# A two-layer hybrid decoder trunk on one core: three normalising steps and two preparation steps change their engine or their place

## The chip, the cores and the metric

The kernel runs on one core of a Trainium2 chip. The metric is the device time of one execution in microseconds (us). TensorE (PE) does matrix products, VectorE (DVE), ScalarE (ACT) and GpSimd (POOL) the elementwise work, and SyncE (SP) issues the transfers. Each engine works through its own list of instructions in order; a wait on one instruction holds everything behind it on that engine.

## What is computed

The reference is a stack of two layers on a sequence of 1024 tokens of width 1024. Layer 0 mixes by an SSD recurrence and MLA attention, layer 1 by GLA and NSA attention; each mixer ends in one output projection, and each layer ends in a SwiGLU FFN. Every sub-layer has the same frame:

```python
for layer in range(DEPTH):
    shift_m, scale_m, gate_m, shift_f, scale_f, gate_f = adaln_modulation(c, *ada[layer])
    h = rmsnorm(x, pre_m) * (1.0 + scale_m) + shift_m
    x = x + gate_m * rmsnorm(mixers[layer](h), post_m)
    h = rmsnorm(x, pre_f) * (1.0 + scale_f) + shift_f
    x = x + gate_f * rmsnorm(swiglu(h, *ffns[layer]), post_f)
```

In layer 0 the mixer projects its input to, among others, a query latent `q_a` (384 wide) and a key-value latent `kv_a` (256 wide); `rmsnorm(kv_a)` is multiplied by `w_kv_b` later, in the MLA attention.

## The kernel before

Tokens are cut into eight tiles of 128. All matrix products are made from two-part numbers: an operand is split into `hi` (rounded to the matmul type, on ACT) and `lo` (the rest, mostly on DVE), and `mm3` issues three matmuls for a product (lines 114, 115 and 116 of the file). PSUM banks are handed out from four small rings: `bk`, `cx`, `sm` and `big`. A scheduler of the language places the instructions of each engine; the program gives it the streams, and `merge` and generators that are advanced with `next` set which step is written next to which.

Four places matter here.

**The latent stage of layer 0** (`mixer0_latent`, L940 to L997). `merge` interleaves two streams by weight: `dense()` makes the query latent by long projections, weight 31, and `kv_norm()` normalises the key-value latent, weight 4. For each half of the tokens `row_bcast` multiplies the identity by four columns of `rkv` on DVE (`diag`, L166) and one matmul with ones (L167) spreads them over the partitions into a bank `sm`; POOL adds the two parts of the latent (`kvn`, L990), DVE multiplies (L991), and ACT and POOL split again.

**The mix and the start of the FFN in both layers** (`mix_tiles`, L1195 to L1229, called by `ffn`). Tile by tile PE makes the output projection into two `bk` banks (24 matmuls), DVE adds the partial sum from before (L1223), ACT takes the sum of squares (`sumsq`, L158, with a read of the accumulator), POOL makes 1/sqrt of it (`rstd`, L151 and L152), DVE applies it with the gate (L522) and adds the residual `xt` (L523). A second sum of squares on ACT, a second `rstd`, and `normalise` (L475, DVE) give the normalised tile `y`. Two tiles later `to_blocks` transposes it on PE (L509), ACT (L495, four instructions) and DVE (L498, L499) modulate it, and the parts go into the operand slabs of the FFN. The FFN's first products are written after the sixth step of `mix_tiles`, between the last tiles.

**The FFN's block sums** (`make_T`, L1245). The FFN multiplies 2x2 blocks by Winograd's scheme with seven products for each block pair. `make_T` is a generator that forms the sums of the input blocks (DVE subtractions over 128 x 2048, L1259's copy on ACT and its rest on DVE). It is advanced by `next(gen)` at the top of the loop over products, at steps 0, 6, 9, 12 and 16. A first product (`p == "1"`) ends with a copy of its bank by ACT (L1378, `nc.scalar.copy`).

**The tail of FFN layer 0** (`ffn_out`, `front` and `back`, from L1690). When the down projection of a tile is done, `front` normalises and adds it like the mix does, and multiplies the new `x` by its `rstd` on ACT (L1718); `back` transposes it (L484), modulates it (L495, L498) and splits it for the next layer.

Of the kernel before, what the change touches and what calls it, by code (L numbers as in the profile page):

```python
# [15 lines left out]
AF = mybir.ActivationFunctionType  # L16
ALU = mybir.AluOpType
# [7 lines left out]
D = 1024  # L25
# [21 lines left out]
class Trunk:  # L47
# [422 lines left out]
        nc.vector.tensor_copy(col, ps[:, :3])  # L470
        return banks, col, shifted, later

    def normalise(self, xt, xn):
        r = self.rstd(self.sumsq(xt), 1, 1.0 / D)
        self.nc.vector.tensor_scalar(xn, xt, r, None, op0=ALU.mult)  # L475

    def to_hT(self, pool, xn, i, a, s, hT):

# [479 lines left out]
    def mixer0_latent(self, hT, keep):  # L958

        nc, I, S = self.nc, self.I, self.S  # L960
        qh, ql = S["q"] = self.t(keep, [P, 3, T], "qhi", F32R), self.t(keep, [P, 3, T], "qlo", F32R)
        kvh, kvl = S["kv"]
        rq = S["rq"] = self.t(keep, [P, NT], "rq")
        with ExitStack() as e:
            tmp = self.pool(e, "lat")
            gq = self.t(tmp, [P, 3], "gq")
            nc.sync.dma_start(gq, I["l0_q_a_norm_g"])

            def dense():
                sq = []  # L970
                for j in range(3):
                    sq.append(self.t(tmp, [P, T], "sq", bufs=3))

                    def each(h, hs, ps):
                        nc.scalar.activation(sq[j][:, hs], ps, AF.Square)
                        nc.scalar.activation(qh[:, j, hs], ps, AF.Copy, scale=gq[:, j:j + 1])
                        nc.vector.scalar_tensor_tensor(ql[:, j, hs], ps, gq[:, j:j + 1], qh[:, j, hs].bitcast(F32),
                                                       op0=ALU.mult, op1=ALU.subtract)
                    yield from self.chunk("l0_w_in", 1 + j, hT, each)
                S["wvpool"] = keep  # L980
                S["wv"] = self.split_w(keep, I["w_v"], tag="wv", bufs=1)
                r = self.rstd(self.token_sumsq(sq, self.sm()), NT, 1.0 / 384)
                nc.gpsimd.tensor_scalar(rq, r, 96 ** -0.5, None, op0=ALU.mult)

            def kv_norm():
                for h, hs in enumerate(HALVES):
                    bc = self.row_bcast(tmp, S["rkv"][:, h * 4:(h + 1) * 4], 4, self.sm())
                    for j in range(2):
                        v = self.t(tmp, [P, 512], "kvn", bufs=2)
                        nc.gpsimd.tensor_tensor(v, kvh[:, j, hs].bitcast(F32), kvl[:, j, hs].bitcast(F32), op=ALU.add)  # L990
                        nc.vector.tensor_tensor(v, v, bc, op=ALU.mult)  # L991
                        self.split(kvh[:, j, hs], kvl[:, j, hs], v, nc.gpsimd)
                        yield 1.0
                self.ropetab = self.rope_tables(keep, tmp)

            self.merge((31.0, dense()), (4.0, kv_norm()))

    def mla(self, pool):
        nc, I, S = self.nc, self.I, self.S
# [208 lines left out]
    def mix_tiles(self, pool, gate, a, s, F, B):  # L1208


        nc, S = self.nc, self.S
        xn = {}
        self.mixp[1] = pool
        for i in range(NT + 2):
            if i < NT:
                hi, lo, y = self.mix_in(i) if i else self.mix0
                if i + 2 < NT:
                    self.mixc.append(self.mix_cat(i + 2))
                xn[i] = y
                ps = [self.bk(), self.bk()]  # L1220
                self.natural(ps, [(hi[:, k, :], lo[:, k, :]) for k in range(4)], self.wb)
                for hs, b in zip(HALVES, ps):
                    nc.vector.tensor_tensor(y[:, hs], y[:, hs], b, op=ALU.add)  # L1223
                xt = self.postnorm(pool, y, i, gate)
                self.store_x(xt, i)
                self.normalise(xt, y)
            if i >= 2:
                self.to_blocks(xn.pop(i - 2), i - 2, a, s, F, B)
            yield  # L1229
# [20 lines left out]
    def make_T(self, F, pool, T):  # L1250


        nc = self.nc
        tt = nc.vector.tensor_tensor
        f11, f12, f21, f22 = F
        room = lambda k, dtype=F32R: self.t(pool, [P, 4, 512], f"T{k}", dtype)

        def pair(src, hi, lo):
            nc.scalar.activation(hi, src, AF.Copy)  # L1259
            tt(lo, src, hi.bitcast(F32), op=ALU.subtract)  # L1260
            return hi, lo
        tt(f11, f12, f11, op=ALU.subtract)
        t2 = room(6, F32)
        tt(t2, f22, f11, op=ALU.subtract)
        T["2"] = pair(t2, room(0), room(1))
        yield
        tt(f12, f22, f12, op=ALU.subtract)
        tt(f21, f21, t2, op=ALU.subtract)
        T["3"] = pair(f12, room(2), room(6))
        yield  # L1270
        T["1"] = pair(f11, room(4), self.slab(4))
        yield
        T["4"] = pair(f21, room(3), self.slab(6))
        yield
        T["b"] = pair(f22, room(5), self.slab(5))
        yield

    def ffn(self, l, near, far, ew):
# [222 lines left out]
        for t, (pm, mt, p) in enumerate(seq):  # L1501
            advance(t)
            if t > 16 and t % 4 == 0:
                self.pump()
            if len(seq) - t in (7, 6, 5, 4, 2):
                next(out)
            if t in (0, 6, 9, 12, 16):
                next(gen)
            st = state.setdefault((pm, mt), {})
            w = W.get(wkey(pm, mt, p))  # L1510
            if p == "1":
                st["x"], u = first(mt, pm, w)
                if pm < self.HEADS:
                    nc.sync.dma_start(uq[mt, pm], u)
                else:
                    ublk[mt, pm] = u
            elif p == "2":
                second(mt, pm, w, st["x"])
                if mt and pm == self.HEADS - 1:
                    reload(0)  # L1520
            elif p == "6":
                ps = self.sm()
                product(ps, w, 0, T["2"], True)
                u = ublk[mt, pm]
                tt(u, u, ps, op=ALU.add)
            elif p == "7":
                ps = st["z"] = self.bk()
                product(ps, w, 1, T["3"], True)
                st["u3"] = blk()
                tt(st["u3"], ublk[mt, pm], ps, op=ALU.add)  # L1530
            elif p == "4":
                if mt == 0 and pm < self.HEADS:
                    cblk[pm] = blk()
                    nc.sync.dma_start(cblk[pm], hid[0, pm])
                if mt and pm + 1 < self.HEADS:
                    reload(pm + 1)
                ps = st["z"]
                product(ps, w, 1, T["4"], False)
                c = st["c21"] = blk()
                tt(c, ublk[mt, pm], ps, op=ALU.add)  # L1540
                if mt == 0:
                    nc.scalar.activation(c, c, AF.Silu)
                else:
                    ptt(c, c, state[pm, 0]["c21"], op=ALU.mult)
                    nc.sync.dma_start(hid[1, pm], c)
            elif p == "5":
                ps = st["v"] = self.bk()
                product(ps, w, 0, T["1"], True)
                c = st["u3"]
                tt(c, c, ps, op=ALU.add)  # L1550
                if mt == 0:
                    nc.scalar.activation(c, c, AF.Silu)
                else:
                    ptt(c, c, state[pm, 0]["u3"], op=ALU.mult)  # L1554
                    nc.sync.dma_start(hid[4, pm], c)
            else:
                ps = st["v"]
                product(ps, w, 0, T["b"], False)
                u = ublk[mt, pm]
                tt(u, u, ps, op=ALU.add)  # L1560
                if mt == 0:
                    nc.scalar.activation(u, u, AF.Silu)
                    state[pm, 0]["u"] = u
                else:
                    g = state.pop((pm, 0))
                    finish(pm, g, u, st["u3"], st["c21"])
                    state.pop((pm, 1))
        self.drain()
        ef.close()
        en.close()  # L1570
# [25 lines left out]
    def ffn_out(self, l, hid, wt, fw, pools):  # L1596
# [116 lines left out]
        def front(i):  # L1713
            yi = y[:, i, :]
            if l == 0:
                xt = self.postnorm(pool, yi, i, m["gf0"])
                self.store_x(xt, i)
                nc.scalar.activation(yi, xt, AF.Copy, scale=self.rstd(self.sumsq(xt), 1, 1.0 / D))  # L1718
            else:
                self.store_x(self.postnorm(pool, yi, i, m["gf1"]), i, True)  # L1720

# [755 lines left out]
```

## Time and profile before

| | us |
|---|---|
| median of 3 runs | 3149.43 |
| range of the runs | 3145.93 to 3151.14 |
| the profiled execution | 3150.23 |
| its span on the core | 3148.5 |
| PE busy | 3025.7 (96%) |
| DVE busy | 2160.0 (69%) |
| ACT busy | 1340.6 (43%) |
| POOL busy | 695.3 (22%) |

The span is the time from the first to the last instruction, 1.7 us less than the execution. The times in all rows below are microseconds from the start of the span. PE's rows carry the clock with them: a 128 x 512 matmul takes 0.39 to 0.40 us when it runs in a stream at the full clock (2.4 GHz), with a new one starting every 0.23 us, and 0.63 us where the granted clock has fallen to the lower level (1.2 GHz), with one starting every 0.43 us.

### The profile page before, as it was taken

The page shows a single profiled execution, that of the slowest core. Times are in us where ns is not written, and L with a number is a line of the kernel's source. Part 1 is how long each engine was busy: PE and PEld are TensorE (multiplying, and loading weights), DVE is VectorE, ACT ScalarE, POOL GpSimd, SP SyncE. Part 2 cuts the span into 40 slices and gives each one's busy share as a digit, 9 for nine tenths or more (in the row PEclk, how much of TensorE's full clock was granted, in tenths as well). Part 3 has the DMA queues.
Part 4 walks back from the last instruction along what each step waited for, and adds up shares of the span by engine and source line. Part 5 has one row for each costly group of instructions (what it writes and reads, how often), then busy time and mean ns, then how long its engine had stood idle before and what let it go on. Part 6 is the DMA issues. An engine that isn't in the chain of part 4 may idle for free. (4 is left out here: it accounts for less than half of the span.)

```text
span 3148.5 us, 43054 instructions
## 1 busy us (share of the span) xinstructions
PE 3025.7 (96%) x15880; PEld 2449.0 (78%) x15880; DVE 2160.0 (69%) x3381; ACT 1340.6 (43%) x2193; POOL 695.3 (22%) x671
## 2 busy tenths in 40 slices
PE   7999989999999999999999999889999899999998
PEld 6877777777787888787888888767777787888787
DVE  5876846767777787666636554677766887778655
ACT  6445435546522223436432432355555632223433
POOL 1003343201034222001213332023222114222001
PEclk9999989999999999999999999899999999999999
DMA  6567433325554556874524333331312655455864
GB/s 222 166 213 220 143 111 101 101 67 186 190 174 160 189 198 234 312 256 139 174 94 154 128 109 112 123 111 53 99 50 92 229 170 182 166 197 208 294 194 160
DMA packets 222866, 510.16 MB, mean 162 GB/s; under 512 B 23824, under 2 KB 62832, under 8 KB 221632
## 3 DMA queue, kind: packets, MB, share of 16 engines
q1 hardware_dynamic: 222656, 507.42, 47.9%
q8 instruction: 125, 2.05, 0.3%
q14 instruction: 85, 0.70, 0.1%
HBM read 370.09 MB, written 137.25 MB: 161 GB/s over the span
## 5 line engine op out<-in xcount | busy, mean ns | idle before, releaser
L115 PE MATMUL bk<-slab,whi 128*128 128x512 f32 x1208 | 481.7, 399 | 1.4 <-DVE slab L145 1.4
L114 PE MATMUL bk<-slab,whi 128*128 128x512 f32 x784 | 327.7, 418 | 6.9 <-ACT whi L132 3.4
L116 PE MATMUL bk<-slab,wlo 128*128 128x512 f32 x784 | 314.3, 401 | 2.4 <-DVE wlo L133 2.4
L115 PEld LDWEIGHTS bk<-slab,whi 128*128 128x128 f32 x1208 | 232.2, 192 | 52.2 <-issue 2.9
L114 PE MATMUL bk<-T,whi 128*128 128x512 f32 x528 | 210.3, 398 | 1.1 <-DVE blk L1530 1.1
L116 PE MATMUL bk<-T,wlo 128*128 128x512 f32 x528 | 207.8, 393 | 0.0
L151 POOL TENSOR_SCALAR rstd<-ss 128x1 f32<-128x1 f32 (+1 forms) x86 | 29.9, 348 | 735.4 <-ACT junk L158 662.3
L114 PEld LDWEIGHTS bk<-slab,whi 128*128 128x128 f32 x784 | 152.6, 195 | 43.9 <-issue 7.0
L116 PEld LDWEIGHTS bk<-slab,wlo 128*128 128x128 f32 x784 | 151.6, 193 | 36.0 <-DVE wlo L133 2.6
L1326 ACT ACTIVATE whi<-rawa 128x512 fp32r<-128x512 f32 (+1 forms) x108 | 80.7, 750 | 196.3 <-PE bk L115 156.9
L114 PE MATMUL cx<-slab,whi 128*128 128x512 f32 x368 | 148.5, 405 | 8.3 <-ACT blk L1378 5.9
L2290 POOL TENSOR_SCALAR pexp<-pexp,rs 128x640 f32<-128x640 f32 (+7 forms) x128 | 95.8, 752 | 245.5 <-DVE rs L2289 91.4
L115 PE MATMUL cx<-slab,whi 128*128 128x512 f32 x368 | 146.8, 399 | 0.2 <-DVE slab L397 0.2
L116 PE MATMUL cx<-slab,wlo 128*128 128x512 f32 x368 | 146.2, 397 | 0.0
L1112 PE MATMUL sm<-ident,pexp 128*128 128x128 f32 x816 | 132.4, 278 | 6.2 <-POOL pexp L2290 2.3
L1554 POOL TENSOR_TENSOR blk<-blk,blk 128x512 f32<-128x512 f32 x22 | 35.2, 1600 | 422.0 <-DVE blk L1550 327.5
L1112 PEld LDWEIGHTS sm<-ident,pexp 128*128 128x128 f32 x816 | 93.5, 140 | 43.8 <-issue 19.5
L1114 ACT COPY pT<-sm 128x512 f32<-128x512 f32 (+2 forms) x144 | 76.4, 530 | 111.8 <-PE sm L1112 110.9
L1327 DVE TENSOR_TENSOR wlo<-rawa,whi 128x512 fp32r<-128x512 f32 (+1 forms) x108 | 118.4, 1096 | 7.0 <-ACT whi L1326 6.2
L114 PEld LDWEIGHTS bk<-T,whi 128*128 128x128 f32 x528 | 99.3, 188 | 26.7 <-DVE blk L1530 1.6
L2286 ACT ACTIVATE pexp<-pexp,nm 128x640 f32<-128x640 f32 (+7 forms) x128 | 93.9, 734 | 61.2 <-DVE nm L2284 45.5
L116 PEld LDWEIGHTS bk<-T,wlo 128*128 128x128 f32 x528 | 99.2, 188 | 24.4
(650 smaller groups left out, 8517.7 us busy)
## 6 DMA issues: line engine op xcount, KB each, us to landing
ada<-in_l_ada_w_dram SPq DMA_DIRECT2D x80, 512.0 KB, 4.7
hid<-blk SPq DMA_DIRECT2D x154, 256.0 KB, 2.0
raw<-in_l_w_in_dram SPq DMA_DIRECT2D x48, 512.0 KB, 3.7
ab<-hid SPq DMA_DIRECT2D x94, 256.0 KB, 3.9
cat<-cat SPq DMA_DIRECT2D x64, 256.0 KB, 2.7
ab<-wt SPq DMA_DIRECT2D x60, 256.0 KB, 4.3
raw<-in_l_w_gate_dram SPq DMA_DIRECT2D x28, 512.0 KB, 4.6
raw<-in_l_w_up_dram SPq DMA_DIRECT2D x28, 512.0 KB, 4.7
```

The lines of the kernel that those rows point to most:

```text
L114: mm(out, lh, rh, start=start, stop=False, skip_group_check=more)
L115: mm(out, lh, rl, start=False, stop=False, skip_group_check=more)
L116: mm(out, ll, rh, start=False, stop=stop, skip_group_check=more)
L151: nc.gpsimd.tensor_scalar(r, ss, inv_d, EPS, op0=ALU.mult, op1=ALU.add)
L1112: nc.tensor.transpose(ps[:, k * P:(k + 1) * P], e[:, (b + k) * P:(b + k + 1) * P], self.ident)
L1114: (nc.scalar.copy if self.evac else nc.vector.tensor_copy)(pt[:, b:b + m, :], ps[:, :m * P].rearrange("p (k c) -> p k c", c=P))
L1326: nc.scalar.activation(hi, src, AF.Copy)
L1327: (eng or nc.vector).tensor_tensor(lo, src, hi.bitcast(F32), op=ALU.subtract)
L1554: ptt(c, c, state[pm, 0]["u3"], op=ALU.mult)
L2286: nc.scalar.activation(e, e, AF.Exp, bias=nm, scale=-1.0, accum_out=rs)
L2290: nc.gpsimd.tensor_scalar(e, e, rs, 0.0, op0=ALU.mult, op1=ALU.add)
```

## The change

There are four edits. The numbers of instructions of each engine stay the same in sum: eight normalising instructions leave ACT in the tail, and eight come to it in the mixes.

1. In the tail of FFN layer 0, `front` calls `normalise`, so the multiplication by `rstd` is a DVE instruction (eight tiles).
2. `kv_norm` begins with an empty step of 1.5, and its weight in `merge` becomes 5.5.
3. In `mix_tiles`, tiles 2 to 5 of both layers are multiplied by `rstd` on ACT (L476 of the new file) and the other four stay on DVE.
4. `make_T` has three more steps, and the FFN's loop advances it behind the product instead of ahead of it, at steps 0, 2, 4, 6, 8, 9, 12 and 16.

```diff
+    def normalise(self, xt, xn, scalar=False):
         r = self.rstd(self.sumsq(xt), 1, 1.0 / D)
-        self.nc.vector.tensor_scalar(xn, xt, r, None, op0=ALU.mult)
+        if scalar:
+            self.nc.scalar.activation(xn, xt, AF.Copy, scale=r)
+        else:
+            self.nc.vector.tensor_scalar(xn, xt, r, None, op0=ALU.mult)
...
             def kv_norm():
+                yield 1.5
...
-            self.merge((31.0, dense()), (4.0, kv_norm()))
+            self.merge((31.0, dense()), (5.5, kv_norm()))
...
-                self.normalise(xt, y)
+                self.normalise(xt, y, 2 <= i < 6)
...
         tt(f11, f12, f11, op=ALU.subtract)
+        yield
         t2 = room(6, F32)
         tt(t2, f22, f11, op=ALU.subtract)
+        yield
         T["2"] = pair(t2, room(0), room(1))
         yield
         tt(f12, f22, f12, op=ALU.subtract)
+        yield
         tt(f21, f21, t2, op=ALU.subtract)
...
-            if t in (0, 6, 9, 12, 16):
-                next(gen)
...
+            if t in (0, 2, 4, 6, 8, 9, 12, 16):
+                next(gen)
...
-                nc.scalar.activation(yi, xt, AF.Copy, scale=self.rstd(self.sumsq(xt), 1, 1.0 / D))
+                self.normalise(xt, yi)
```

Four places show how the order moves. In the orders a name is a tile or a buffer, and a trailing x3 counts equal rows; lines of the new file are higher by 3 to 7 (its L498 is L495 before, L1263 is L1259, L1333 is L1326, L1385 is L1378).

PE in the latent stage, before: the first broadcast matmul (`diag` is the identity times the latent's `rstd`) stands inside the first of the token halves' streams of projections.

```order
L116 MATMUL bk_3056<-slab_21_108,wlo_3053 128x512
L114 MATMUL bk_3056<-slab_21_108,whi_3052 128x512
L115 MATMUL bk_3056<-slab_22_109,whi_3052 128x512
L167 MATMUL sm_3063<-diag_535_3064,ones_83 128x512
L116 MATMUL bk_3056<-slab_21_108,wlo_3053 128x512
L114 MATMUL bk_3056<-slab_21_108,whi_3052 128x512
```

PE at the same place after the change:

```order
L114 MATMUL bk_3084<-slab_25_112,whi_3052 128x512
L115 MATMUL bk_3084<-slab_26_113,whi_3052 128x512
L116 MATMUL bk_3084<-slab_25_112,wlo_3053 128x512
L167 MATMUL sm_3103<-diag_536_3104,ones_83 128x512
L114 MATMUL bk_3084<-slab_25_112,whi_3052 128x512
L115 MATMUL bk_3084<-slab_26_113,whi_3052 128x512
```

The broadcast has moved back by 22 matmuls, from row 1244 to row 1266 of PE's list; the second one moves back by 24.

ACT in the mix of layer 0, tiles 3 and 4, before (`xt` is the new residual, `my` the tile that is normalised, `slab` and `mhi` are operands of the next products):

```order
L158 ACTIVATE junk_7050,ss_7049<-xt_7037 128x1024
L144 ACTIVATE slab_1411_6813<-slab_1414_6816 128x4x128
L495 ACTIVATE slab_1415_6817<-sm_7131,shift_2180,scale_3354 128x128
L158 ACTIVATE junk_7115,ss_7114<-my_1475_7076 128x1024
L495 ACTIVATE slab_1415_6817<-sm_7131,shift_2180,scale_3354 128x128 x2
L144 ACTIVATE slab_1409_6811<-slab_1415_6817 128x4x128
L144 ACTIVATE mhi_7369<-mcat_7157 128x512
```

ACT there after the change:

```order
L498 ACTIVATE slab_1415_6817<-sm_7131,shift_2180,scale_3354 128x128 x4
L158 ACTIVATE junk_7050,ss_7049<-xt_7037 128x1024
L144 ACTIVATE slab_1409_6811<-slab_1415_6817 128x4x128
L476 ACTIVATE my_1459_7001<-xt_7037,rstd_1472_7052 128x1024
L158 ACTIVATE junk_7115,ss_7114<-my_1475_7076 128x1024
L144 ACTIVATE slab_1411_6813<-slab_1414_6816 128x4x128
L144 ACTIVATE mhi_7369<-mcat_7157 128x512
```

The normalising instruction stands between the sum of squares of `xt` of one tile, from which its own `rstd` comes, and the sum of squares of the next tile's `my`.

ACT at the start of the FFN of layer 0, before (L1378 copies a product's bank, L1259 copies a block sum, L1326 splits a weight tile):

```order
L1378 COPY blk_7595<-cx_7582 128x512
L1259 ACTIVATE T_1608_7763<-slab_1415_6817 128x2048
L1326 ACTIVATE whi_7568<-rawa_7552 128x1024
L1326 ACTIVATE T_1577_7572<-rawa_7554 128x1024
L1259 ACTIVATE T_1579_7578<-T_1578_7576 128x2048
L1378 COPY blk_7619<-cx_7606 128x512
```

ACT there after the change:

```order
L1385 COPY blk_7588<-cx_7575 128x512
L1263 ACTIVATE T_1610_7779<-slab_1415_6817 128x2048
L1333 ACTIVATE whi_7568<-rawa_7552 128x1024
L1333 ACTIVATE T_1577_7572<-rawa_7554 128x1024
L1385 COPY blk_7613<-cx_7600 128x512
L1263 ACTIVATE T_1595_7678<-T_1587_7633 128x2048
L1393 ACTIVATE blk_7631<-cx_7575 128x512
L1333 ACTIVATE whi_7638<-rawa_7556 128x1024
L1333 ACTIVATE whi_7658<-rawa_7558 128x1024
L1263 ACTIVATE T_1606_7759<-slab_1413_6815 128x2048
L1385 COPY blk_7675<-cx_7662 128x512
```

The second product's copy stands ahead of the second block sum's copy; the third product's copy has two weight splits and a block sum ahead of it.

ACT in the tail of FFN layer 0, one tile, before (`hv` is a modulated tile; `y` is the tile of the down projection):

```order
L158 ACTIVATE junk_12144,ss_12143<-xt_12131 128x1024
L495 ACTIVATE hv_12212<-sm_12207,shift_11166,scale_11762 128x128
L1718 ACTIVATE y_10586<-xt_12131,rstd_2226_12146 128x1024
L158 ACTIVATE junk_12191,ss_12190<-y_10586 128x1024
L144 ACTIVATE slab_2209_12057<-hv_12167 128x4x128
L495 ACTIVATE hv_12212<-sm_12207,shift_11166,scale_11762 128x128 x3
```

ACT there after the change:

```order
L158 ACTIVATE junk_12144,ss_12143<-xt_12131 128x1024
L498 ACTIVATE hv_12212<-sm_12207,shift_11166,scale_11762 128x128
L158 ACTIVATE junk_12191,ss_12190<-y_10586 128x1024
L498 ACTIVATE hv_12212<-sm_12207,shift_11166,scale_11762 128x128 x3
L144 ACTIVATE slab_2209_12057<-hv_12167 128x4x128
L144 ACTIVATE slab_2207_12055<-hv_12212 128x4x128
```

The two sums of squares, of this tile's `xt` and of the next tile's `y`, have one short instruction between them instead of that and L1718. PE's order is otherwise the same up to the pieces around these places: in both mixes 8 to 12 matmuls of the first FFN products change places with transposes of tile 4 and later, and in both FFN starts the second half of a product pair comes earlier.

## Rows read from the trace of the kernel before

**Rows 1.** Timeline of PE, latent stage: start, duration, engine, line, tiles, [idle before <-releaser].

```profile
371.11 0.39 PE L115 MATMUL bk<-slab,whi 128*128 128x512 f32 x1
375.14 2.04 PE L167 MATMUL sm<-diag,ones 128*128 128x512 f32 x2 [3.64 <-DVE diag L166]
...
378.14 0.39 PE L116 MATMUL bk<-slab,wlo 128*128 128x512 f32 x1
...
389.29 1.02 PE L167 MATMUL sm<-diag,ones 128*128 128x512 f32 x2
```

**Rows 2.** Timeline of DVE in the same stretch, from the wait's cause on.

```profile
370.48 4.51 DVE L166 TENSOR_SCALAR diag<-ident,rstd 128x128 f32<-128x128 f32 x4 [2.06 <-POOL rstd L152]
```

**Rows 3.** Table of stretches: length, busy time by engine, granted clock (PEclk), DMA.

```profile
834.60:839.10 4.50, 4.50 (x13) 3.54 (x14) 3.92 (x4) 3.28 (x4) 0.00 (x0) 0.62 0.84 290
...
1474.00:1481.00 7.00, 6.26 (x16) 4.91 (x17) 3.29 (x6) 5.73 (x11) 2.00 (x4) 0.54 0.43 152
...
2464.00:2471.00 7.00, 5.79 (x17) 3.80 (x16) 6.50 (x9) 4.72 (x11) 1.67 (x4) 0.54 0.61 197
```

**Rows 4.** Waits of PE from 745 to 800, mix of layer 0.

```profile
PE bk L114 <- ACT junk L158: 2.4, 1, 2.4
PE sm L509 <- DVE slab L498: 1.6, 1, 1.6
PE sm L509 <- DVE slab L145: 1.0, 1, 1.0
```

**Rows 5.** Timeline of DVE, one cycle of the mix of layer 0.

```profile
780.50 1.28 DVE L522 SCALAR_TENSOR_TENSOR my<-my,rstd,gp 128x1024 f32<-128x1024 f32 x1
...
787.78 1.28 DVE L522 SCALAR_TENSOR_TENSOR my<-my,rstd,gp 128x1024 f32<-128x1024 f32 x1
```

**Rows 6.** Timeline of ACT and PE, start of the FFN of layer 0.

```profile
829.98 1.06 ACT L1326 ACTIVATE whi<-rawa 128x1024 fp32r<-128x1024 f32 x1 [0.61 <-DMA rawa<-in_l_w_gate_dram]
...
832.17 1.89 ACT L1259 ACTIVATE T<-T 128x2048 fp32r<-128x2048 f32 x1
833.97 0.56 ACT L1378 COPY blk<-cx 128x512 f32<-128x512 f32 x1
...
834.59 0.50 PE L114 MATMUL cx<-slab,whi 128*128 128x512 f32 x1 [2.65 <-ACT blk L1378]
```

**Rows 7.** Lines grouped: durations min/median/max in ns of the two normalising forms.

```profile
L1718 ACT ACTIVATE y<-xt,rstd x8: 1136/1150/1153, 1439.3 to 1491.0; 128x1024 f32<-128x1024 f32 x8
...
L475 DVE TENSOR_SCALAR my<-xt,rstd x16: 752/754/755, 757.3 to 2498.5; 128x1024 f32<-128x1024 f32 x16
```

**Rows 8.** Waits of PE from 1425 to 1515, tail of FFN layer 0.

```profile
PE sm L484 <- ACT hv L495: 4.8, 3, 2.8
PE sm L484 <- DVE hv L498: 2.9, 4, 1.5
PE bk L114 <- ACT slab L144: 2.6, 1, 2.6
PE bk L115 <- DVE slab L145: 1.4, 1, 1.4
```

**Rows 9.** Timeline of ACT, one cycle of the tail.

```profile
1457.56 1.06 ACT L158 ACTIVATE junk<-xt 128x1024 bf16<-128x1024 f32 x1 [1.78 <-DVE xt L523]
...
1459.65 1.15 ACT L1718 ACTIVATE y<-xt,rstd 128x1024 f32<-128x1024 f32 x1 [0.60 <-POOL rstd L152]
...
1465.84 1.06 ACT L158 ACTIVATE junk<-xt 128x1024 bf16<-128x1024 f32 x1 [1.78 <-DVE xt L523]
```

**Rows 10.** Waits of PE from 2445 to 2530, mix and FFN start of layer 1.

```profile
PE cx L114 <- ACT blk L1378: 3.2, 1, 3.2
PE sm L509 <- DVE my L475: 2.0, 2, 1.3
PE sm L509 <- DVE slab L498: 1.6, 2, 1.1
PE cx L114 <- ACT slab L144: 1.2, 1, 1.2
```

More of the change, by code (lines that the diff above doesn't have):

```diff
@@ L471, in first_h @@
         return banks, col, shifted, later
-    def normalise(self, xt, xn):
+    def normalise(self, xt, xn, scalar=False):
         r = self.rstd(self.sumsq(xt), 1, 1.0 / D)
-        self.nc.vector.tensor_scalar(xn, xt, r, None, op0=ALU.mult)
+        if scalar:
+            self.nc.scalar.activation(xn, xt, AF.Copy, scale=r)
+        else:
+            self.nc.vector.tensor_scalar(xn, xt, r, None, op0=ALU.mult)
     def to_hT(self, pool, xn, i, a, s, hT):
```

## The prediction

> **What bounds the kernel now.** I read the busy times first: PE works 3025.7 of a span of 3148.5 us, so only PE's idle time, some 120 us, and its time at the lower clock can be gained; ACT, DVE and POOL matter only where PE waits for them. None of the four edits adds or removes work on PE. So I went through the waits of PE at the places that the edits touch, then through the timelines there, and last through the granted clock of the stretches behind the waits. The reader is to see six places.
>
> In the latent stage PE stands 3.64 us in front of the broadcast matmul, for DVE's `diag` [rows 1]. DVE takes 4.51 us for four small multiplications there [rows 2]. In the mix of layer 0 three waits are 5.0 us, for the tile's second `rstd` chain and for DVE's modulation [rows 4]. At the start of the FFN of layer 0 PE waits 2.65 us for a copy of a bank; that copy is behind a 1.89 us block-sum copy on ACT [rows 6]. In the tail the waits of PE sum to 11.7 us [rows 8]. Layer 1 has the same two places as layer 0, with 4.8 us in its mix and 3.2 us at its FFN start [rows 10]. Behind three of these places the granted clock falls to 0.62, 0.54 and 0.54, a mixture of the two levels [rows 3]. A stretch of 7.0 us at 0.54 does the work of 3.8 us, so 3.2 us are lost in each of the last two; at 0.62 for 4.5 us 1.7 us are lost. What the rows show is that each of these falls comes after a stretch in which PE had waited.
>
> **Edit 2, the latent norm.** From the matmul that starts at 371.11 to the one at 378.14, 7.03 us, PE did four 128 x 512 starts and the broadcast [rows 1]. In the stream behind it 49 starts take 389.29 - 378.14 = 11.15 us, 0.2275 each; the second broadcast, for which nothing waits, has 1.02 us. So the work was 4 x 0.2275 + 1.02 = 1.93 us and 5.1 us were lost: 3.64 of wait, the rest slow issue and the lower clock behind it. After the change the broadcast stands 22 matmuls later, so PE comes to it at about 371.34 + 22 x 0.2275 = 376.3. DVE's `diag` starts when `rstd` arrives, which the edit does not touch, and is done by 370.48 + 4.51 = 375.0 [rows 2]. Margin 1.3 us. What hides `diag` now is the 22 matmuls themselves; without them the old wait is back. The normalised latent is first read by the value products, which stand far behind in PE's order. Gain 5.1; if `diag` comes 3 us later than before, 1.7 of wait return and with them some of the low clock: 3.0 as the small end. No DMA is moved past anything.
>
> **Edit 3, the mix of layer 0.** On DVE the instruction takes 0.754 us, on ACT the same form takes 1.150 [rows 7]. So 0.4 us longer for each tile, in a chain that also holds a sum of squares on ACT, two POOL steps and the transposes. The new order puts it between two sums of squares, and it waits for a `rstd` that comes from the first: the next tile's sum of squares, and with it the next L522, is held back by that wait and by the 1.15. I followed the order with the durations of the trace: tile 3's L522 comes 0.9 us later than before, tile 4's 2.0 and tile 5's 1.0 later, where the cycle was 7.28 [rows 5]. Against this DVE is rid of 0.75 us in each cycle, ACT's four modulations are ahead of the sum of squares, and PE has first FFN products ahead of the transposes of tile 4. The slab of tile 3 is complete 3.6 us earlier. Of PE's 5.0 us of waits [rows 4] two remain about 1.3 each in this replay. Gain 2.5, between a loss of 1.0, where ACT's chain sets the cycle, and the whole 5.0. The store and the load of `xt` that are issued behind go up to 2.3 us later, and have slack.
>
> In **layer 1** the same replay gives tile 2's transposes 0.4 us later (ACT's longer instruction), the second half of them 0.6 earlier (DVE is free), tile 3's 0.3 earlier and tile 4's sum of squares 0.8 later. Of 4.8 us of waits [rows 10] about 3.8 stay, and with them the clock's fall at 2464. Gain 1.0; between a loss of 1.0 and 4.2, the 1.0 with the 3.2 of the clock.
>
> A rule stands on each side of this edit. The row shows 754 against 1150 ns, 0.4 us more for each of eight tiles, 3.2 us if all lay on PE's path. The Trainium skill, page "ScalarE: Activation LUTs", section "Rules for kernel authors", says that multiplications belong on VectorE and not on ScalarE. Its page "Perfetto Trace Analysis", section "Optimizing Scalar/DVE Operations", allows such a move to ScalarE where DVE is saturated. The trace agrees with the first in the durations; by that rule alone the edit would cost up to 3.2 us where I take a gain of 3.5.
>
> **Edit 4, the FFN's start.** In layer 0 ACT now copies the second product's bank ahead of the 1.89 us block sum, so the copy starts at 832.17 instead of 833.97 [rows 6] and PE resumes 1.80 us earlier. The wait before it shrinks to 0.9 us, and the clock has less reason to fall: 1.7 us [rows 3] come back in the forecast. Then the new order charges: the third product's copy stands behind two weight splits of 1.06 and a block sum of 1.89, and PE needs that bank sooner; I get a new wait of 0.9 to 1.05. Gain 1.8 + 1.7 - 1.05 = 2.45. Small end 0, where the new wait is as long as the old; large end 3.5 without it. The block sums themselves, spread over more steps, are still ahead of the products that read them. In layer 1 the loss is 3.2 of wait [rows 10] and a fall of the clock of about the same size as in layer 0, 4.9 together; the same share of it as in layer 0 (2.45 of 4.35) is 2.75. Ends 0 and 4.2.
>
> **Edit 1, the tail.** One cycle of ACT takes 1465.84 - 1457.56 = 8.28 us [rows 9]. In it L1718 waits 0.60 us for its `rstd`, then runs, and only then the sum of squares of the next tile starts: 0.60 + 1.06 (from its start to the next start) = 1.66 us that the next tile's chain has no need of. On DVE the multiplication takes 0.754 [rows 7] and nothing of the next tile's chain on ACT waits for it. The cycle becomes 6.6 us. PE's own work for a tile is less than that, so it still waits, but less. Replayed, the wait for the slab that ended at 1474.74 ends 4.4 us earlier. Whether the fall of the clock right behind it (3.2 us) [rows 3] goes with it is open: waits of 0.6 and 1.6 remain before it. I take a third of it: 5.5. Ends 2.0 (DVE late with the multiplication, as its part in the waits of 2.9 [rows 8] allows) and 7.6. The closing wait of 2.6 stays, since it hangs on the last tile.
>
> **Sum.** 5.1 + 2.5 + 1.0 + 2.45 + 2.75 + 5.5 = 19.3 us. The profiled execution was 3150.2 us, 0.8 above the median of 3149.4, so 3131 in that execution's terms and 3130 in the median's. I say 3131. The stages between the places are paced by PE at 0.2275 us for a matmul and keep their order, so a gain is passed on.
>
> **Rivals.** *The waits move only.* In the mixes and the FFN starts the same in-order queues of ACT and DVE end a few instructions later; only the latent (5.1) and half of the tail (2.75) are gained: 3142. For it speaks that ACT has the next waits in line everywhere (L495, L1378); against it that the copy at 833.97 has only one instruction of 1.89 ahead of it that matters.
>
> *All falls of the clock go.* Then the large ends hold: 5.1 + 5.0 + 4.2 + 3.5 + 4.2 + 7.6 = 29.6, so 3121. Against it: waits of over 1 us are left before two of the three falls.
>
> *ScalarE is the wrong place for edit 3.* Nothing is gained in the two mixes and 3.2 us of longer instructions are paid: the other 15.8 less 3.2, 12.6, so 3137.5. That is what the first rule of the skill would give.
>
> *Slower: ACT's chain sets the mix.* Place: between the two sums of squares on ACT in the mixes. Price: for each of eight tiles the wait for `rstd` (0.85, of which DVE's 0.4 wait is a part) and 1.04 of the instruction, 15 us, with falls of the clock of 1.7 and 3.2 behind, 20 us; with nothing gained at the FFN starts, and 10.6 gained by the latent and the tail, 9 us more than before: 3159. It decides once the cycle from L522 to L522 goes from 7.28 [rows 5] to over 8.5 in all four tiles. For it: two of three replayed tiles are late by 0.9 and 2.0. Against it: the third is late by 1.0 only, so delays do not add up, and PE has 22 other matmuls in between.
>
> **How the numbers follow.** Forecast (3125 to 3136) 0.43; all clock falls go (3121) 0.20; waits move only (3142) 0.18; ScalarE wrong (3137.5) 0.11; slower (3159) 0.08. A measurement of this kernel tells changes of over about 0.2%, 6.3 us, from none: the borders are 3143.1 and 3155.7. Half of the third case's spread lies within the border, and a little of the fourth's: same 0.11, slower 0.07, faster 0.82. The range takes in the large ends of the costs below and reaches above to the cases of 3142: 3114 to 3146.
>
> **What would show it.** Right: no wait of PE at L167 and a stream of 0.23 us starts around it; the cycle of sums of squares in the tail near 6.6 us; the first copy L1378 behind the first block sum at the start of the FFN ahead of the second; PE's waits in the mix of layer 0 under 3.5 us. Wrong: the cycle of the mix over 8 us with waits of PE for the new ACT instruction; a granted clock near 0.54 still behind the tail's wait with 7 us of length; a copy of a bank in the FFN start that PE waits for as long as before.

## The result, and the profile after

The changed kernel takes 3128.28 us (median, 3124.21 to 3130.22); the ratio to the kernel before is 0.9937, with an interval of 0.9925 to 0.9949. That is 19.8 us of 3149, between 16 and 24. Run once more beside other kernels it had 0.9946 (0.9935 to 0.9958), 17.0 us. The forecast was 3131, a gain of 18.4 against the median.

To see where it came from, the same matmul was looked up in both traces (before and after the change) and its two starts compared. Ahead of the latent stage the new execution is already 1.5 us early, with no edit there. The shift then grows place by place (the last column is the mean granted clock of TensorE in the place, before and after):

| place | shift at its start | shift at its end | gain there | forecast | clock |
|---|---|---|---|---|---|
| latent stage | -1.5 (353.82 to 352.30) | -6.8 (396.08 to 389.26) | 5.3 | 5.1 | 0.96, 1.00 |
| mix of layer 0 | -8.0 (749.10 to 741.09) | -10.9 (799.98 to 789.11) | 2.9 | 2.5 | 0.97, 1.00 |
| FFN start of layer 0 | -10.9 | -13.1 (970.23 to 957.14) | 2.2 | 2.45 | 0.98, 1.00 |
| tail of FFN layer 0 | -15.0 (1327.10 to 1312.15) | -19.2 (1505.00 to 1485.81) | 4.2 | 5.5 | 0.97, 0.98 |
| mix of layer 1 | -20.3 (2413.24 to 2392.92) | -21.6 (2479.93 to 2458.34) | 1.3 | 1.0 | 0.95, 0.97 |
| FFN start of layer 1 | -21.6 | -23.4 (2542.41 to 2519.05) | 1.8 | 2.75 | 0.97, 1.00 |

The six places sum to 17.7 us; the other 5 us of this execution lie between them, where no edit is. In part they are the clock's: around 1323 the granted clock of before is down for 7 us (0.76), in the new execution it is 1.00 there, 1.7 us. The 1.5 us ahead of the latent stage are mostly shorter waits of PE (21.4 us before, 20.1 after). Two executions of the changed kernel, compared with each other in the same way, differ by up to 2 us ahead of the mix alone, so such differences are not put down to the edits. In all six places the clock is higher too, so a part of each gain is the clock's and not the shorter wait's.

The waits of PE at the places of [rows 4], [rows 8] and [rows 10], and at both FFN starts, after the change (columns: engine, line, who is waited for, us in total, times, longest). The mix of layer 0, 735 to 800:

```profile
PE sm L512 <- ACT slab L498: 1.4, 1, 1.4
PE cx L114 <- ACT slab L144: 1.3, 1, 1.3
PE bk L114 <- DVE my L1227: 0.8, 1, 0.8
PE bk L116 <- DVE mlo L145: 0.4, 1, 0.4
PE sm L512 <- ACT my L476: 0.2, 1, 0.2
```

The FFN start of layer 0, 805 to 850:

```profile
PE cx L114 <- ACT blk L1385: 1.6, 2, 0.9
PE cx L114 <- DVE blk L1395: 0.2, 1, 0.2
```

The tail, 1405 to 1505:

```profile
PE bk L114 <- ACT slab L144: 3.2, 2, 2.9
PE bk L115 <- DVE slab L145: 2.4, 2, 1.9
PE sm L487 <- DVE hv L501: 2.2, 4, 0.8
PE sm L487 <- ACT hv L498: 1.2, 1, 1.2
```

The mix and the FFN start of layer 1, 2415 to 2515:

```profile
PE sm L512 <- ACT my L476: 2.8, 2, 1.7
PE cx L114 <- ACT blk L1385: 2.0, 2, 1.3
PE bk L114 <- ACT mhi L144: 1.5, 1, 1.5
PE bk L114 <- DVE my L1227: 0.9, 1, 0.9
PE cx L114 <- DVE blk L1395: 0.3, 1, 0.3
```

In the latent stage there is no wait of PE left (3.64 us before). The tail's sum fell from 11.7 to 9.0, the FFN starts' from 2.65 to 1.8 and from 3.2 to 2.3. In the mix of layer 0 it fell from 5.7 to 4.1, with a wait of 0.7 for `mlo` that [rows 4] leave out. In the mix of layer 1 PE waits no less than before, 5.2 against 4.8 us: most of DVE's names have gone and ACT's have come. Together the waits fell by 9 us, half of the 17.7.

### The profile page after: what moved, and what is told of

It reads as the page before. It is cut to its first block, busy times and chain, and to the rows that moved or that the text cites. A ratio compares the mean times of both kernels' runs of the same rounds, so it can differ in the third digit from the quotient of the medians.

```text
span 3126.1 us, 43054 instructions
## 1 busy us (share of the span) xinstructions
PE 3012.5 (96%) x15880; PEld 2439.1 (78%) x15880; DVE 2157.5 (69%) x3381; ACT 1338.9 (43%) x2193; POOL 698.4 (22%) x671
## 5 line engine op out<-in xcount | busy, mean ns | idle before, releaser
L1333 ACT ACTIVATE whi<-rawa 128x512 fp32r<-128x512 f32 (+1 forms) x108 | 80.4, 750 | 195.3 <-PE bk L115 162.1
```

## The experiments

Medians and ratios are to the kernel before, on the same chip and in the same rounds. Four kernels have one edit each.

**Edit 2 alone.**

```diff
             def kv_norm():
+                yield 1.5
...
-            self.merge((31.0, dense()), (4.0, kv_norm()))
+            self.merge((31.0, dense()), (5.5, kv_norm()))
```

> Edit 2 alone (the empty first step and the weight 5.5 of the latent norm). Theory: PE meets the broadcast matmul L167 22 matmuls later and no longer waits for diag; the 5.1 us lost between 371.1 and 378.1 come back there, the first diag group still takes about 4.5 us, and every other stage keeps its waits: about 3144 us. Rival (the gain is another stage's luck with the clock): the L167 wait is gone, but the time moves by less than 3 us, because the projections' stream ends at the same time as before. Rival (waits move only): a wait of 1 us or more stands at a consumer of the latent behind 400.

Measured: 0.9981 (0.9971 to 0.9990), 6.0 us. No wait for `diag`; the broadcast starts at 376.41, where the forecast put it (376.3). A matmul that started at 395.63 before starts at 390.00: 5.6 us, the forecast's 5.1 and little more. Behind 400 PE's waits for DVE's `V` sum to 1.5 us, as they do before the change, so the wait has not moved there. DVE's `diag` takes 4.56 us (4.51 before), now out of sight:

```profile
370.56 4.56 DVE L166 TENSOR_SCALAR diag<-ident,rstd 128x128 f32<-128x128 f32 x4 [2.06 <-POOL rstd L152]
...
376.41 1.02 PE L167 MATMUL sm<-diag,ones 128*128 128x512 f32 x2
```

So the theory holds, and both rivals fall: that the gain was another stage's luck, and that the wait only moved.

**Edit 3 alone.**

```diff
-                self.normalise(xt, y)
+                self.normalise(xt, y, 2 <= i < 6)
```

> Edit 3 alone (tiles 2 to 5 of both mixes normalised on ACT). Theory: 2.5 to 3 us gained in the mix of layer 0 and about 1 in layer 1, together 3.5 to 4: about 3146 us; PE waits of 0.2 to 1.7 us for the new ACT instruction appear, and more than that goes from DVE's. Rival (multiplication is ScalarE's wrong work): nothing gained or up to 3.2 us lost, 3149 to 3153. Rival (ACT's chain sets the cycle): cycle of L522 over 8.5 us, 3160 or more.

Measured: 0.9988 (0.9979 to 0.9997), 3.8 us. The waits of PE in the mix of layer 0 are the five of the changed kernel (1.4, 1.3, 0.7, 0.4, 0.2). In this execution the clock still falls behind them (0.63 from 784 to 788), and the place gains 1.1 us only; in the changed kernel's execution it doesn't and the place gains 2.9. In the mix of layer 1 it is the other way: the clock does not fall in this execution, and the place gains 2.6, not 1. The theory's size holds in sum (between 1 and 7 us), not place by place; the rival of "nothing or a loss" does not hold.

**Edit 4 alone.**

```diff
         tt(f11, f12, f11, op=ALU.subtract)
+        yield
         t2 = room(6, F32)
         tt(t2, f22, f11, op=ALU.subtract)
+        yield
...
         tt(f12, f22, f12, op=ALU.subtract)
+        yield
...
-            if t in (0, 6, 9, 12, 16):
+            if t in (0, 2, 4, 6, 8, 9, 12, 16):
                 next(gen)
```

(The new line stands behind the product, the old one ahead of it.)

> Edit 4 alone (three more steps of the block sums, advanced behind the product). Theory: at each FFN start the wait of 2.65 or 3.2 us becomes two or three waits of together 1.8 to 2.3, and the fall of the clock behind it goes: 2.5 in layer 0 and 2.5 in layer 1, about 3144.5 us. Rival (waits only move): the new waits sum to as much as the old ones and the clock falls as before: 3149.

Measured: 0.9986 (0.9977 to 0.9995), 4.4 us. In layer 0 the waits are 1.9 and 0.3, 2.2 us, and the clock doesn't fall; by 950 the place has gained 1.5 us. In layer 1 this execution has a wait of 1.79 us, longer than the 1.27 of the changed kernel, and behind it the clock does fall; the place gains less than 0.5 us:

```profile
2508.84 0.50 PE L114 MATMUL cx<-slab,whi 128*128 128x512 f32 x1 [1.79 <-ACT blk L1381]
```

```profile
2508.00:2513.00 5.00, 4.16 (x12) 3.30 (x13) 4.16 (x4) 4.03 (x5) 0.00 (x0) 0.68 0.81 284
```

The first is a line of PE's timeline, the second of the table of stretches, with the granted clock, 0.68, behind POOL's column. The theory held in layer 0 for the waits and the clock, with a smaller gain than its 2.5, and not in layer 1, where the waits sum to 2.5 and the fall stays. What decides whether the clock falls behind such a wait is not shown.

**Edit 1 alone.**

```diff
-                nc.scalar.activation(yi, xt, AF.Copy, scale=self.rstd(self.sumsq(xt), 1, 1.0 / D))
+                self.normalise(xt, yi)
```

> Edit 1 alone (tail's multiplication by rstd on DVE). Theory: the cycle of sums of squares of the tail goes from 8.28 to about 6.6 us, the waits for ACT's modulation shrink, 4.4 to 5.5 us gained: about 3144 to 3145 us. Rival (the closing wait and the clock take it back): the tiles come earlier but the fall of the clock at the end of the tail is as long as before, 2 us gained: 3147.

Measured: 0.9981 (0.9972 to 0.9990), 6.0 us; the tail itself gains 4.3 by the starts of its matmuls. The cycle is 7.0, not 6.6 us (6.2 to 7.3 over the tail). In the changed kernel (timeline of ACT, the sums of squares of `xt`, which answer to [rows 9]):

```profile
1448.98 1.06 ACT L158 ACTIVATE junk<-xt 128x1024 bf16<-128x1024 f32 x1 [2.66 <-DVE xt L526]
...
1455.98 1.06 ACT L158 ACTIVATE junk<-xt 128x1024 bf16<-128x1024 f32 x1 [2.38 <-DVE xt L526]
...
1462.99 1.06 ACT L158 ACTIVATE junk<-xt 128x1024 bf16<-128x1024 f32 x1 [2.37 <-DVE xt L526]
```

ACT now idles 2.4 us in each cycle until DVE has the next `xt`, and DVE works 6.17 of the 7.00 us from 1448.98 to 1455.98. Four edits alone sum to 20.2 us (each uncertain by about 3), all together 17.0 and 19.8: within that uncertainty the edits add up, and none is seen to feed on another's gain.

**The changed kernel once more, without edit 3, and with all eight tiles on ACT.** These three and the next ran side by side.

> The changed kernel once more, beside the next three on one chip. All theories: ratio 0.993 to 0.995 to the kernel before.

Measured 0.9946 (0.9935 to 0.9958).

```diff
-                self.normalise(xt, y, 2 <= i < 6)
+                self.normalise(xt, y)
```

> The changed kernel without edit 3 (all eight tiles of both mixes normalised on DVE). Theory (DVE is the full engine of the mix): 3.5 to 5 us slower than the changed kernel, PE's waits in the mix of layer 0 are about 5.7 us again instead of 4.1. Rival (multiplication belongs on VectorE): as fast as the changed kernel or up to 3 us faster.

Measured: 0.9964 (0.9953 to 0.9976), 5.7 us slower than the changed kernel beside it by the ratios, 4.6 by the medians; the two intervals overlap by a hair. By the starts of the matmuls the two mixes gain 0.3 and 0.4 us against the kernel before, where the changed kernel gains 2.9 and 1.3. The waits of the mix of layer 0 are those of [rows 4] again:

```profile
PE bk L114 <- ACT junk L158: 2.4, 1, 2.4
PE sm L509 <- DVE slab L498: 1.6, 1, 1.6
PE sm L509 <- DVE slab L145: 1.0, 1, 1.0
PE bk L116 <- DVE mlo L145: 0.5, 1, 0.5
```

```diff
-                self.normalise(xt, y, 2 <= i < 6)
+                self.normalise(xt, y, True)
```

> The changed kernel with all eight tiles of both mixes normalised on ACT. Theory (a balance of the two in-order engines): within 2 us of the changed kernel, since the tiles 0, 1, 6 and 7 stand where PE has other work. Rival (DVE full, so the more on ACT the better): 2 to 4 us faster. Rival (ACT's chain sets the cycle): 3 us or more slower, with waits of PE for the ACT instruction of 1 us and more at tiles 0 and 1.

Measured: 0.9954 (0.9942 to 0.9966), 2.5 us above the changed kernel by the ratios, within both intervals. Its mix of layer 0:

```profile
PE bk L114 <- DVE my L1227: 3.1, 1, 3.1
PE sm L512 <- ACT slab L498: 2.0, 2, 1.2
PE bk L116 <- DVE mlo L145: 0.4, 1, 0.4
```

One long wait of 3.1 us stands for the product's bank. The likely reason, which no run separates, is that with more tiles on ACT the next tile's sum of squares is later and L525 and L1227 with it. In layer 0 none on ACT and all on ACT both leave 5.5 us of waits, the four leave 4.1, so there the four in the middle are a balance. In layer 1 it is not so: all on ACT leaves 4.2 us of waits where the four leave 5.2, and in this execution, without a fall of the clock, the place gains 4.1; the four gain 1.3 there, and 2.5 in an execution without a fall. That the same four are best for both layers was not tried.

**The second bank copy ahead of two weight splits.** In the changed kernel ACT's list at the FFN start of layer 0 runs so (timeline):

```profile
819.13 1.06 ACT L1333 ACTIVATE whi<-rawa 128x1024 fp32r<-128x1024 f32 x1 [0.57 <-DMA rawa<-in_l_w_gate_dram]
820.44 1.06 ACT L1333 ACTIVATE T<-rawa 128x1024 fp32r<-128x1024 f32 x1 [0.25 <-DMA rawa<-in_l_w_up_dram]
821.40 0.57 ACT L1385 COPY blk<-cx 128x512 f32<-128x512 f32 x1
821.87 1.92 ACT L1263 ACTIVATE T<-T 128x2048 fp32r<-128x2048 f32 x1
```

The copy stands behind two splits that wait for their weights' transfers, though it needs neither. The edit, on the changed kernel:

```diff
-            while todo and need[todo[0]] - t <= 6:
+            while todo and need[todo[0]] - t <= (2 if t < 2 else 6):
```

> The changed kernel with two weight splits at each FFN start written later (a look-ahead of 2 instead of 6 products in the first two steps), so that the second product's bank copy stands ahead of them on ACT. Theory (the wait that is left there, 0.90 and 1.27 us, is the copy held behind splits that wait for their weights' transfer): both waits go, 2 us less than the changed kernel, and the later wait of 0.7 stays. Rival (the wait is due to the block sums on ACT and DVE): the wait stays, or comes back as long one product later, within 0.5 us.

Measured: 0.9953 (0.9941 to 0.9965), not told apart from the changed kernel. The order is as meant, and both first waits are gone:

```profile
820.26 0.57 ACT L1385 COPY blk<-cx 128x512 f32<-128x512 f32 x1
821.09 1.06 ACT L1333 ACTIVATE whi<-rawa 128x1024 fp32r<-128x1024 f32 x1 [0.27 <-DMA rawa<-in_l_w_gate_dram]
...
825.83 0.50 PE L114 MATMUL cx<-slab,whi 128*128 128x512 f32 x1 [0.20 <-ACT blk L1393]
...
830.00 0.50 PE L114 MATMUL cx<-slab,whi 128*128 128x512 f32 x1 [1.14 <-ACT blk L1385]
```

The third product's wait has grown from 0.71 to 1.14, and a new one of 0.20 stands between. The sum of the FFN start's waits goes from 1.8 to 1.5 in layer 0 and from 2.3 to 1.4 in layer 1, 1.2 us in all, which the runs can't tell from none. The first wait also differs between two executions of the changed kernel, 0.90 and 1.51 in layer 0, so such a sum is known to half a microsecond at best. The cause of the first wait is shown, and the theory's 2 us are not: more than a third of it was handed on to the next copies.

**The latent's addition on DVE, in the kernel before.**

```diff
-                        nc.gpsimd.tensor_tensor(v, kvh[:, j, hs].bitcast(F32), kvl[:, j, hs].bitcast(F32), op=ALU.add)
+                        nc.vector.tensor_tensor(v, kvh[:, j, hs].bitcast(F32), kvl[:, j, hs].bitcast(F32), op=ALU.add)
```

> The kernel before, with the latent's addition (kvn, L990) on DVE instead of POOL and nothing else. Theory (the first multiplication of diag takes 3.0 us because POOL's addition runs at the same time, not because of its own work): the four take about 1.1 us, the broadcast waits less than 0.5 us, and about 4 to 5 us are gained as by edit 2: 3144 to 3145 us. Rival (diag is slow by itself, as the first of its kind): the four take 4.5 us as before, the wait of 3.6 stays, and the time stays within 1 us or rises by DVE's additions.

Measured: 0.9987 (0.9975 to 0.9998), 4.1 us. The four multiplications take 2.25 us instead of 4.51, between the two theories' numbers, and the broadcast waits 1.38 instead of 3.64:

```profile
372.43 2.25 DVE L166 TENSOR_SCALAR diag<-ident,rstd 128x128 f32<-128x128 f32 x4 [2.06 <-POOL rstd L152]
...
372.34 1.81 POOL L607 MEMSET ropetab<- 128x2048 f32 x1
...
374.83 1.10 PE L167 MATMUL sm<-diag,ones 128*128 128x512 f32 x2 [1.38 <-DVE diag L166]
```

With the additions gone from POOL, its next instruction, a clearing of a table (1.81 us), came up to the same moment. Both theories had overlooked it; the last section shows that it stood beside `diag` before as well. So the length of `diag` is POOL's doing: what runs there beside it sets how long it takes.

**DVE's splits of the tail on POOL, in the changed kernel.**

```diff
-            self.split(hT[h][0][q][:, :, c:c + P], hT[h][1][q][:, :, c:c + P], v)
+            self.split(hT[h][0][q][:, :, c:c + P], hT[h][1][q][:, :, c:c + P], v, None if q else nc.gpsimd)
```

> The changed kernel with the lower parts of the tail's first four blocks (L145 for q = 0, eight tiles) on POOL instead of DVE. Theory (after the change DVE's own list sets the tail's cycle of 7.0 us, two thirds of it work): DVE loses 0.6 us in each cycle, the cycle goes to about 6.4 and the time down by 2 us or so to the changed kernel. Rival (POOL's in-order list and its sharing with DVE): the rstd steps on POOL stand behind an addition of 1.3 us and more, the cycle goes to 7.5 or more, and the time rises by 2 us or more.

Measured: 0.9960 (0.9946 to 0.9974), about 4 to 7 us slower than the changed kernel (0.9946 and 0.9937 in its two measurements; the interval of the first overlaps). Its tail gains 0.7 us against the kernel before, where the changed kernel gains 4.2. The rival holds. The sums of squares of `xt` start at 1437.86, 1446.18, 1454.14 and 1460.82, cycles of 8.3, 8.0 and 6.7 us, and while POOL works on its split DVE's instruction takes 2.30 us where it takes 1.28 elsewhere:

```profile
1450.07 2.30 DVE L525 SCALAR_TENSOR_TENSOR y<-y,rstd,gp 128x1024 f32<-128x1024 f32 x1 [0.44 <-POOL rstd L152]
...
1450.01 1.28 POOL L145 TENSOR_TENSOR slab<-hv,slab 128x512 fp32r<-128x512 f32 x1
```

So DVE's list could not be relieved in this way, and whether a shorter list of DVE would bring the cycle under 7.0 stays open.

## Why the prediction was right, point by point

**The latent stage** came out as worked out: with edit 2 alone the broadcast is met at 376.41 against 376.3 and `diag` is done 1.3 us ahead of it, the margin of the forecast. The place gains 5.3 us by the same two matmuls, with edit 2 alone as in the changed kernel. The clock that had fallen behind the wait (0.75 from 376 to 380) is 1.00 there in the changed kernel.

**The mix of layer 0.** The replay forecast L522 of three tiles 0.9, 2.0 and 1.0 us later than before against an equal start. In the changed kernel (timeline of DVE; L525 is L522 of before):

```profile
757.63 1.29 DVE L525 SCALAR_TENSOR_TENSOR my<-my,rstd,gp 128x1024 f32<-128x1024 f32 x1 [0.44 <-POOL rstd L152]
...
766.11 1.29 DVE L525 SCALAR_TENSOR_TENSOR my<-my,rstd,gp 128x1024 f32<-128x1024 f32 x1 [0.72 <-ACT slab L498]
...
774.40 1.28 DVE L525 SCALAR_TENSOR_TENSOR my<-my,rstd,gp 128x1024 f32<-128x1024 f32 x1 [1.07 <-POOL rstd L152]
...
781.14 1.28 DVE L525 SCALAR_TENSOR_TENSOR my<-my,rstd,gp 128x1024 f32<-128x1024 f32 x1 [0.72 <-POOL rstd L152]
```

The cycles are 8.48, 8.29 and 6.74. Before, the same instruction started at 765.62 and 773.22 and then as in [rows 5]. The execution is 8.0 us early at this place, so the first of the four compares with 765.62 and is on time, and the next three are 0.9, 1.9 and 1.4 us late. The rival of ACT's chain was near in two cycles of three: its 8.5 was all but reached, and "over 8 us" had been named as a sign of being wrong. It did not decide, since the third cycle caught up; that PE had other products to do meanwhile is the prediction's argument, which no run tested.

Two waits of about 1.3 us were forecast, and 1.4 and 1.3 are there. The replay missed two others, 0.8 and 0.2: of the 5.0 us of [rows 4] 3.7 remain, not 2.6, and with the wait for `mlo` the sum is 4.1, over the 3.5 that had been named as a sign of being right. So the waits gave 1.3 us where the sum had 2.5. The rest of the 2.9 is a fall of the clock behind 787, which the sum left out:

```profile
787.00:791.00 4.00, 3.90 (x13) 2.77 (x14) 3.88 (x6) 2.25 (x7) 0.66 (x2) 0.57 0.69 193
```

In the changed kernel the clock stays up there; in the run with the tail's splits on POOL, whose edit lies in the tail alone and whose five waits in this mix are the same within 0.1 us, it falls:

```profile
774.00:784.00 10.00, 7.88 (x33) 5.38 (x31) 8.88 (x11) 6.97 (x13) 2.26 (x5) 1.00 0.59 207
```

```profile
778.00:782.00 4.00, 4.00 (x12) 3.17 (x13) 3.28 (x5) 3.03 (x6) 1.89 (x4) 0.60 0.45 154
```

The same five waits stand in five executions. In two (the changed kernel, twice) the clock stays up and the place gains 2.9; in three (edit 3 alone, the later weight splits, the tail's splits on POOL) it falls and the place gains 1.1 to 1.4. That the place came out near 2.5 is luck: the term for the waits was too large by a little over 1 us, and the clock gave 1.7 that nobody had counted.

Two rules of the Trainium skill on this edit can now be weighed. The row still has ACT at 1.150 us for the instruction where DVE takes 0.754, and edit 3 gains all the same: 3.8 us alone, between 1 and 7, and 4.6 to 5.7 within the changed kernel, where the intervals just overlap. The rule of the Trainium skill, page "ScalarE: Activation LUTs", section "Rules for kernel authors", that multiplications belong on VectorE, is right on the duration of one and was wrong on the time here; the advice of its page "Perfetto Trace Analysis", section "Optimizing Scalar/DVE Operations", to offload from a saturated DVE agrees with these runs for half of the tiles (DVE is busy 43.0 of the 50.9 us of this place before the change). That more tiles give more is not shown (0.9954 against 0.9946).

**The mix of layer 1** gained its 1.3 for another reason than the one given. The sum said that 3.8 us of waits stay and the clock's fall with them. The waits are 5.2, more than before; the fall got milder: the stretch around it, 2444 to 2451, has 0.76 where before had 0.54 for as long a time [rows 3], 1.5 us. The step that failed is the term for the waits, mis-sized by 1.4: tile 2's and 3's transposes wait 2.8 us for ACT's L476 itself. That the gain came near the 1.0 is luck, as the two errors cancel. With the tail's splits on POOL the same mix has no fall, and the place gains 2.5.

**The FFN starts.** In layer 0 the two waits were forecast at 0.9 and 0.9 to 1.05, and are 0.90 and 0.71 (1.51 and 0.73 in the second execution of the changed kernel); the clock's 1.7 came back. The place's 2.2 flatter the forecast, though: by 950 it has gained 1.4, and 0.8 comes from a fall of the clock at 968 in the kernel before, far behind the start. In layer 1 the share taken from layer 0 was too large by 1 us; in edit 4 alone the clock fell there and the place gained next to nothing. The prediction named the queue of ACT for the new wait, and the experiment with the later splits shows the cause of the first one that is left: the copy stood behind two splits that waited for their weights.

**The tail** was forecast 1.3 us too high. The term that was mis-sized is the replayed 4.4: the wait for the slab that ended at 1474.74 ends 3.3 us earlier, in the changed kernel and with edit 1 alone. L1718's 1.66 us left ACT's cycle, but DVE's list, longer by 0.75 and busy 6.17 us of it, became the likely bound: its cycle is 7.0, not 6.6. This was the term's own small-end reason, DVE late with the multiplication; what sat on the path were `xt` (L526) and the slabs' lower parts (L145), for which PE now waits 2.4 us. The fall behind 1474, of which the sum had counted a third, is gone in this execution and half there in the second one of the changed kernel (0.66 from 1456 to 1461); the fall at the end of the tail is longer (0.67 from 1480 to 1490, where before had 0.66 from 1500 to 1505). The closing wait stayed, 2.9 against 2.6.

**The sum** of the places is 17.7 against 19.3, and the medians give 17.0 to 19.8 against 18.4. The latent stage and the tail hold from execution to execution (5.3, and 4.2 to 5.3 where the splits stay on DVE); the mixes and the FFN starts move by 1 to 2 us with the clock, so that the sum came this close is in part luck. Of the rivals, the large ends (all falls of the clock go) fell, since those in the mix of layer 1 and at the tail's end are still there; "waits move only" fell for the tail and layer 0, and holds for the mix of layer 1, whose waits moved from DVE to ACT and did not shrink.

## What to carry to other kernels

Where PE waits once and the producer is merely late, move the consumer behind work that is ready: 22 matmuls cost nothing and hid 3.6 us. Where two in-order engines share a chain, a longer instruction on the idler one can pay, until its own list closes the cycle; follow the order tile by tile with the durations of the trace, since this gave the two longest waits of the first mix to 0.1 us, though it missed two short ones of 1.0 in sum. The clock's share behind a wait could not be forecast to better than all or nothing: before crediting it to an edit, compare the same place over several executions.

## What the runs showed of the hardware

How much POOL lengthens DVE's instructions was unexpected. The grouped line of `diag` in the kernel before, 370 to 376, and with the additions taken off POOL:

```profile
L166 DVE TENSOR_SCALAR diag<-ident,rstd x4: 268/1590/3036, 370.5 to 374.7; 128x128 f32<-128x128 f32 x4
```

```profile
L166 DVE TENSOR_SCALAR diag<-ident,rstd x4: 269/968/1798, 372.4 to 374.4; 128x128 f32<-128x128 f32 x4
```

In the kernel before POOL worked beside it without a break (timeline):

```profile
370.41 2.50 POOL L990 TENSOR_TENSOR kvn<-kvhi,kvlo 128x512 f32<-128x512 f32 x2
372.86 1.80 POOL L607 MEMSET ropetab<- 128x2048 f32 x1
```

The same instruction takes 0.27 us alone. Before, the first of the four takes 1.30 beside POOL's first addition (1.29), the second 3.04, from 371.70 on, beside the second addition and the clearing (1.26 and 1.80), and the third 1.88 beside the clearing. With the additions away, the longest is 1.80 beside the clearing of 1.81. The Trainium skill, page "SBUF — State Buffer", section "SBUF: two separate sides", says that GpSimd and DVE share a pair of ports: whichever starts first, a GpSimd instruction or a DVE instruction that needs the pair (in a two-port mode, or with two inputs in SBUF against a GpSimd instruction that reads there), holds it for its whole length and the other is blocked. The trace agrees in the durations, and adds that DVE was held over two of POOL's instructions in a row. In which mode `diag` runs no trace shows.

Falls of the clock came and went between executions, and not with the wait ahead of them alone. In the kernel before PE waits 2.69 us until 967.49, and the granted clock is 0.57 from 968 to 972; in the changed kernel it waits 2.68 us at the same matmul, and the clock is 1.00 from 955 to 959. The stretch 1322 to 1329 has 0.76 before, behind a wait of 0.9 us that the changed kernel's two executions don't have, and they have no fall there. What decides stays open.
